# Where the parting copies, transposes and joining copies of gated rows are issued in a decoder layer's SwiGLU

## The chip, the cores and the metric

The kernel runs on one core of a Trainium2 chip. The metric is the device time of one execution in microseconds. The engines are named as the profile names them: PE (TensorE), DVE (VectorE), ACT (ScalarE), POOL (GpSimd) and SP (SyncE, which here only issues DMAs).

## The reference

One decoder layer in fp32 on 256 tokens, with D_MODEL = 2048 and D_FF = 5632:

```python
def swiglu(x, w_gate, w_up, w_down):
    return (jax.nn.silu(x @ w_gate) * (x @ w_up)) @ w_down
...
h = h + 0.5 * swiglu(rmsnorm(h, g_ffn1[l]), w1_gate[l], w1_up[l], w1_down[l])
z = rmsnorm(h, g_mix[l]) @ w_in[l]
y_a = spatial_gating(z[..., :o_q], g_v[l], w_s[l], b_s[l])
y_b = window_attention_sinks(z[..., o_q:o_k], z[..., o_k:o_v], z[..., o_v:], sinks[l])
y = jnp.concatenate([rmsnorm(y_a, g_a_out[l]), rmsnorm(y_b, g_b_out[l])], axis=-1)
h = h + y @ w_out[l]
h = h + cross_attention(rmsnorm(h, g_x[l]), rmsnorm(mem, g_mem[l]), w_xq[l], w_xkv[l], w_xo[l])
h = h + 0.5 * swiglu(rmsnorm(h, g_ffn2[l]), w2_gate[l], w2_up[l], w2_down[l])
return rmsnorm(h, g_final)
```

The change concerns the two SwiGLU blocks, FFN1 and FFN2.

## The kernel before

**Products.** Every fp32 operand x is split into a rounded high part and a low part (`split`, L146 to L148): ACT casts the high part (L147) and DVE subtracts it from x for the low part (L148). A product is then three passes on PE: high by high, low by high, high by low. Tile names say which part is meant: wh and wl are the parts of a weight chunk, th and tl those of sums of weight blocks, afh and afl those of activations.

**Chunks and units.** Weights come in chunks of 1 MB (`load`, L307 ff): one DMA on SP's queue (L318 or L341) fills a raw buffer of which there are three; wh and wl have two buffers each, the sums' tiles one each. A chunk is plain (N), or it is multiplied by one of two Strassen-like schemes (C and S). An S chunk needs sums of its weight blocks: DVE makes them in three steps (L320, L323, L324), and then its halves (T1 with T3, T2 with T4) are split, each with a 1024-wide cast of th on ACT and a 1024-wide subtract of tl on DVE. Its own weights need a 1536-wide cast and subtract, those of N and C chunks 2048-wide ones. Eight chunks make a unit, whose products accumulate in PSUM banks (matmuls at L411). In FFN1 the gate and up products are 11 units c = 0 to 10 (tiles f1g...): unit 0 has plain chunks, units 2 to 9 the kinds "SCSCSCSC". FFN2 (f2g...) has 11 units of C and S chunks. The down products are four units of each FFN (f1d..., f2d...), with the kinds of `KINDS_D`.

**What sets the order.** `push` loads a chunk and calls `turn` with the chunk's matmuls; `turn` emits the matmuls of the chunk before and, at a unit's end, what follows from its result. `turn` also keeps the list `later`: an entry (n, f) has f called n chunks after it was put there, 0 meaning at once in the same turn. So a unit's end is worked off in the first chunks of the next unit, which are called its head here. The order on PE is pinned as it is written. The order on ACT, DVE, POOL and SP is made by a scheduler from the order of the code and its dependencies, so an instruction can be issued earlier or later than it is written.

**From a gate unit to the down products.** At a gate unit's end, DVE and ACT combine its banks (L561 to L572), apply SiLU (L688) and multiply by the up half (L692 or L694). The result is gated rows of two token blocks, 128 tokens each, with tokens on partitions. The down products need them with channels on partitions. `rows_done` (L655 to L685) does this for each unit: per token block a parting copy on ACT (L664, tile f1w or f2w) separates the 16-bit halves of the fp32 numbers, and a transposing DMA on SP's queue (L669, tile f1t or f2t) turns them; then four joining copies on ACT (L677, tile f1a or f2a), one for each of two halves q and two token blocks, put the halves together again. Each q makes one chunk of activations, `acts[2 * c + q]`, which `inner` takes in the down stage (and for the first few already in unit 10): `fill` (L200 ff) adds or subtracts its blocks and splits it into afh and afl. Before the change both parting copies and both transposes are written at a unit's end (`later` 0) and all four joins two chunks later (`later` 2).

**FFN1's beginning.** In units 0 and 1 of FFN1 the normalized input n1 is still being prepared beside the products: activations at L249 and L910, casts and subtracts of n1fh and n1fl.

Of the kernel before, what the change touches and what calls it, by code (L numbers as in the profile page):

```python
# [10 lines left out]
U16 = mybir.dt.uint16  # L11
# [6 lines left out]
TB = 2  # L18
# [15 lines left out]
def layer_kernel(  # L34
# [22 lines left out]
    nc = tc.nc  # L57
# [13 lines left out]
    def nm(s):  # L71
        uid[0] += 1
        return f"{s}_{uid[0]}"

    def m4(s):
        return mid.tile([P, 1024], F32, tag="m4", name=nm(s))

    def s2(s):
        return tmp.tile([P, 512], F32, tag="s2", name=nm(s))
# [39 lines left out]
    h = const.tile([P, TB, D], F32, name="h")  # L119
# [103 lines left out]
    def laid(kind, k, tb):  # L223
        return BASE[kind].index(f"A{tb + 1}{k + 1}")
# [234 lines left out]
    later = []  # L459
# [95 lines left out]
    KINDS_D = "NNSNSNSN" + "NSNSNSN" + "NNSNSNN"  # L555
# [96 lines left out]
    def ffn(s, get, rs, wgu, wd, on_block, first=None, on_token_block=None):  # L652
        acts = [None] * 22
        pairs = [None] * 22

        def rows_done(c, rows_):
            a = m4(s + "a")
            words = a.bitcast(U16).rearrange("p (q i t h) -> p q i t h", q=2, i=4, h=2)
            halves_ = []

            def turned():
                for tb in range(TB):
                    w = s2(s + "w").bitcast(U16)
                    nc.scalar.copy(  # L664
                        w.rearrange("p (h c) -> p h c", h=2),
                        rows_[tb].bitcast(U16).rearrange("p (c h) -> p h c", h=2),
                    )
                    t = s2(s + "t").bitcast(U16)
                    nc.sync.dma_start_transpose(t.rearrange("p (b r) -> p b r", b=8), w)  # L669
                    halves_.append(t.rearrange("p (h b t) -> p b t h", h=2, b=4))  # L670

            def joined():
                for q in range(2):
                    kind = KINDS_D[2 * c + q]
                    for tb in range(TB):
                        i, j = laid(kind, 0, tb), laid(kind, 1, tb)
                        nc.scalar.copy(  # L677
                            words[:, q, i:j + 1:j - i], halves_[tb][:, 2 * q:2 * q + 2]
                        )
                    acts[2 * c + q] = a[:, q * 512:(q + 1) * 512].rearrange(  # L680
                        "p (k t) -> p k t", k=4
                    )

            later.append((0, turned))
            later.append((2, joined))  # L685

        def gated(up, sg, r, tb):
            nc.scalar.activation(  # L688
# [15 lines left out]
        def gu_unit(c):  # L704
            got = {}

            def late(u):
                r = rs()
                c22 = s2(s + "u")
                at = {(0, 0): got["p1"], (1, 1): c22, (0, 1): got["v"], (1, 0): got["z"]}  # L710
                seven_late(u, got, lambda tb, j: at[tb, j])
                gated(at[0, 1], (at[0, 0], at[0, 0]), r, 0)
                gated(c22, (at[1, 0], at[1, 0]), r, 1)
                rows_done(c, (at[0, 0], at[1, 0]))

            kinds = MORE if 2 <= c <= 9 else FEWER
            order = range(8)
            if c == (first is not None):
                order = ORDER[first is None]
            u = Unit(s + "g", "".join(kinds[j] for j in order))  # L720
            for i in range(8):
                push(
                    u, i, wgu[order[i], c], lambda j=order[i]: get(j),
                    lambda i=i: (
                        i == u.kinds.rindex("S") and seven_early(u, got), i == 7 and late(u)
                    ),
                    beside=lambda i: (
                        first[2](8 + i) if first is not None and c == 1
                        else rs() if (c, i) == (0, 5) else inner(i - 5) if c == 10 and i >= 5 else None
                    ),  # L730
                )

        def plain_gu_unit(c):
            pairs_, before, prep, rs0 = first
            u = Unit(s + "g", "N" * 8, alone=(7,))
            u.gate_first = True

            def late():
                r = rs0()
                sg = [s2(s + "sg") for _ in range(TB)]  # L740
                for tb, (g, up) in enumerate((("P2", "Q3"), ("Q4", "R"))):
                    gated(u[up], (u[g], sg[tb]), r, tb)
                rows_done(c, sg)

            pieces = {0: (1, 0, 3, 2), 1: (1, 3, 0, 2)}
            for i in range(8):
                push(
                    u, i, wgu[i, c], lambda i=i: have(pairs_, i), late if i == 7 else None,
                    pieces=pieces.get(i), beside=prep, before=before,
                )  # L750
# [747 lines left out]
```

## Time and profile before

| | us |
|---|---|
| median of three timed runs (2054.82 to 2057.21) | 2055.46 |
| the profiled execution | 2053.67 |
| its span, first to last instruction | 2051.8 |
| granted TensorE clock, as a share of full speed | 0.999 |
| HBM read, MB | 398.52 |
| DVE busy in tl subtracts of FFN1's gate units (L148, 76 of 1219 ns) | 92.5 |
| ACT idle ahead of the joins of FFN1, waiting for f1t (9 times) | 20.1 |
| ACT idle ahead of the joins of FFN2, waiting for f2t (10 times) | 10.2 |

The profile follows one execution. A row of a timeline has the start, the duration, the engine, the line in the code, the operation and its tiles, and in brackets how long the engine had been idle just before and what ended that idle time. Durations of neighbouring instructions on ACT and DVE overlap a little at their ends, so the distance between two starts is somewhat less than a duration. PEld is the loading of weights into TensorE, beside PE's matmuls.

### The profile page before, as it was taken

The page shows a single profiled execution, that of the slowest core. Times are in us where ns is not written, and L with a number is a line of the kernel's source. Part 1 is how long each engine was busy: PE and PEld are TensorE (multiplying, and loading weights), DVE is VectorE, ACT ScalarE, POOL GpSimd, SP SyncE. Part 2 cuts the span into 40 slices and gives each one's busy share as a digit, 9 for nine tenths or more (in the row PEclk, how much of TensorE's full clock was granted, in tenths as well). Part 3 has the DMA queues.
Part 4 walks back from the last instruction along what each step waited for, and adds up shares of the span by engine and source line. Part 5 has one row for each costly group of instructions (what it writes and reads, how often), then busy time and mean ns, then how long its engine had stood idle before and what let it go on. Part 6 is the DMA issues. An engine that isn't in the chain of part 4 may idle for free.

```text
span 2051.8 us, 24290 instructions
## 1 busy us (share of the span) xinstructions
PE 2021.7 (99%) x9235; PEld 1672.0 (81%) x9235; DVE 1859.9 (91%) x1998; ACT 1293.0 (63%) x1432; POOL 34.4 (2%) x57
## 2 busy tenths in 40 slices
PE   9999999999999999999999999999999999999998
PEld 8777777778888888888888888888888888888886
DVE  6999999989998987989888987799999999999988
ACT  7866666666655675655546765676666667675554
POOL 0000000000000010200000000000000000000000
PEclk9999999999999999999999999999999999999999
DMA  8566666566555565544555553556666666656563
GB/s 312 191 202 219 202 209 213 188 216 215 207 202 207 200 240 179 200 176 168 186 187 186 183 176 134 185 179 221 215 210 231 215 215 207 234 200 219 186 220 129
DMA packets 106884, 413.72 MB, mean 202 GB/s; under 512 B 53376, under 2 KB 55440, under 8 KB 59664
## 3 DMA queue, kind: packets, MB, share of 16 engines
q1 hardware_dynamic: 104320, 405.04, 56.7%
q0 software_dynamic: 2016, 6.30, 0.9%
q8 instruction: 72, 1.18, 0.2%
q10 hardware_dynamic: 432, 0.84, 0.1%
q14 instruction: 44, 0.36, 0.0%
HBM read 398.52 MB, written 2.10 MB: 195 GB/s over the span
## 4 chain that ended last, share of the span: by engine, by line
PE 85%; DVE 5%; ACT 5%; DMA 3%; issue 2%; SPq 0%; POOL 0%; POOLq 0%; DVEq 0%; ACTq 0%
PE f2gQ L411 14%; PE f1gQ L411 11%; PE f2dQ L411 6%; PE f1dQ L411 5%; PE f2gP L411 5%; PE f1gP L411 4%; PE xqQ L411 3%; PE f2dP L411 3%; PE f1dP L411 2%; PE woQ L411 2%; PE xoQ L411 2%; PE f2dR L411 2%; ACT f1gwh L147 2%; PE vQ L411 2%; PE mv0Q L411 2%
## 5 line engine op out<-in xcount | busy, mean ns | idle before, releaser
L148 DVE TENSOR_TENSOR f1gwl<-f1gw,f1gwh 128x1536 fp32r<-128x1536 f32 (+2 forms) x94 | 181.8, 1935 | 37.6 <-ACT f1gwh L147 37.0
L148 DVE TENSOR_TENSOR f2gwl<-f2gw,f2gwh 128x1536 fp32r<-128x1536 f32 (+1 forms) x88 | 179.2, 2038 | 8.1 <-ACT f2gwh L147 7.5
L147 ACT CAST f2gwh<-f2gw 128x1536 fp32r<-128x1536 f32 (+1 forms) x88 | 150.6, 1711 | 48.9 <-PE f2gQ L411 32.6
L147 ACT CAST f1gwh<-f1gw 128x1536 fp32r<-128x1536 f32 (+2 forms) x94 | 153.0, 1628 | 40.8 <-PE f1gQ L411 14.7
L147 ACT CAST f1gth<-f1gt 128x1024 fp32r<-128x1024 f32 x76 | 79.7, 1051 | 90.4 <-DVE f1gt L320 59.0
L411 PE MATMUL f2gQ<-f2gwh,n4fh 128*128 128x512 f32 x317 | 123.7, 390 | 0.2 <-DVE f2gv L570 0.2
L411 PE MATMUL f2gQ<-f2gwh,n4fl 128*128 128x512 f32 x317 | 123.4, 389 | 0.0
L147 ACT CAST f2gth<-f2gt 128x1024 fp32r<-128x1024 f32 x82 | 85.2, 1049 | 56.0 <-DVE f2gt L324 30.7
L147 ACT CAST f2dwh<-f2dw 128x2048 fp32r<-128x2048 f32 (+1 forms) x44 | 77.3, 1758 | 58.5 <-PE f2dQ L411 37.3
L411 PE MATMUL f1gQ<-f1gwh,n1fl 128*128 128x512 f32 x286 | 111.4, 390 | 1.6 <-DVE n1fl L148 1.6
L411 PE MATMUL f1gQ<-f1gwh,n1fh 128*128 128x512 f32 x286 | 111.6, 390 | 0.0
L147 ACT CAST f1dwh<-f1dw 128x2048 fp32r<-128x2048 f32 (+1 forms) x44 | 77.2, 1757 | 49.0 <-PE f1dQ L411 31.6
L148 DVE TENSOR_TENSOR f1dwl<-f1dw,f1dwh 128x2048 fp32r<-128x2048 f32 (+1 forms) x44 | 92.0, 2093 | 10.1 <-ACT f1dwh L147 10.0
L148 DVE TENSOR_TENSOR f2dwl<-f2dw,f2dwh 128x2048 fp32r<-128x2048 f32 (+1 forms) x44 | 92.1, 2093 | 10.0 <-ACT f2dwh L147 9.9
L148 DVE TENSOR_TENSOR f2gtl<-f2gt,f2gth 128x1024 fp32r<-128x1024 f32 x82 | 99.8, 1220 | 1.0
L411 PE MATMUL f2gQ<-f2gwl,n4fh 128*128 128x512 f32 x317 | 96.6, 389 | 0.0
L148 DVE TENSOR_TENSOR f1gtl<-f1gt,f1gth 128x1024 fp32r<-128x1024 f32 x76 | 92.5, 1219 | 2.3 <-ACT f1gth L147 1.7
L411 PE MATMUL f1gQ<-f1gwl,n1fh 128*128 128x512 f32 x286 | 86.9, 389 | 0.0
L411 PEld LDWEIGHTS f2gQ<-f2gwh,n4fh 128*128 128x128 f32 x317 | 59.5, 188 | 12.9 <-DVE f2gv L570 0.6
L411 PEld LDWEIGHTS f2gQ<-f2gwh,n4fl 128*128 128x128 f32 x317 | 59.5, 188 | 12.4
L411 PEld LDWEIGHTS f2gQ<-f2gwl,n4fh 128*128 128x128 f32 x317 | 59.4, 188 | 12.3
L411 PE MATMUL f1gQ<-f1gth,n1fh 128*128 128x512 f32 x152 | 60.1, 395 | 8.7 <-ACT f1gth L147 8.7
(823 smaller groups left out, 6067.1 us busy)
## 6 DMA issues: line engine op xcount, KB each, us to landing
f2gw<-in_w_gu SPq DMA_DIRECT2D x88, 1024.0 KB, 4.9
f1gw<-in_w_gu SPq DMA_DIRECT2D x86, 1024.0 KB, 4.9
f1dw<-in_w_down SPq DMA_DIRECT2D x44, 1024.0 KB, 4.8
f2dw<-in_w_down SPq DMA_DIRECT2D x44, 1024.0 KB, 4.8
wow<-in_w_out SPq DMA_DIRECT2D x16, 1024.0 KB, 4.9
xqw<-in_w_xq SPq DMA_DIRECT2D x16, 1024.0 KB, 4.8
xow<-in_w_xo SPq DMA_DIRECT2D x16, 1024.0 KB, 4.8
qw<-in_w_in SPq DMA_DIRECT2D x8, 1024.0 KB, 4.8
```

The source lines that it names most:

```text
L147: nc.scalar.copy(hi, src)
L148: nc.vector.tensor_tensor(lo, src, hi.bitcast(F32), ALU.subtract)
L411: nc.tensor.matmul(self.banks[name], x, y, start=name not in self.begun, stop=self.left[name] == 0)
```

## The change

The code in `rows_done` is divided by token block and by half. The parting copy and the transposing DMA of token block tb are now written 1 + tb chunks after the unit's end, and the two joining copies of half q 4 + q chunks after it. Number and shape of the operations stay as they are.

```diff
-            def turned():
+            def turned(tb):
+                w = s2(s + "w").bitcast(U16)
+                nc.scalar.copy(
+                    w.rearrange("p (h c) -> p h c", h=2),
+                    rows_[tb].bitcast(U16).rearrange("p (c h) -> p h c", h=2),
+                )
+                t = s2(s + "t").bitcast(U16)
+                nc.sync.dma_start_transpose(t.rearrange("p (b r) -> p b r", b=8), w)
+                halves_.append(t.rearrange("p (h b t) -> p b t h", h=2, b=4))
+
+            def joined(q):
+                kind = KINDS_D[2 * c + q]
                 for tb in range(TB):
-                    w = s2(s + "w").bitcast(U16)
-                    nc.scalar.copy(
-                        w.rearrange("p (h c) -> p h c", h=2),
-                        rows_[tb].bitcast(U16).rearrange("p (c h) -> p h c", h=2),
-                    )
-                    t = s2(s + "t").bitcast(U16)
-                    nc.sync.dma_start_transpose(t.rearrange("p (b r) -> p b r", b=8), w)
-                    halves_.append(t.rearrange("p (h b t) -> p b t h", h=2, b=4))
-
-            def joined():
-                for q in range(2):
-                    kind = KINDS_D[2 * c + q]
-                    for tb in range(TB):
-                        i, j = laid(kind, 0, tb), laid(kind, 1, tb)
-                        nc.scalar.copy(
-                            words[:, q, i:j + 1:j - i], halves_[tb][:, 2 * q:2 * q + 2]
-                        )
-                    acts[2 * c + q] = a[:, q * 512:(q + 1) * 512].rearrange(
-                        "p (k t) -> p k t", k=4
-                    )
-
-            later.append((0, turned))
-            later.append((2, joined))
+                    i, j = laid(kind, 0, tb), laid(kind, 1, tb)
+                    nc.scalar.copy(words[:, q, i:j + 1:j - i], halves_[tb][:, 2 * q:2 * q + 2])
+                acts[2 * c + q] = a[:, q * 512:(q + 1) * 512].rearrange("p (k t) -> p k t", k=4)
+
+            for tb in range(TB):
+                later.append((1 + tb, lambda tb=tb: turned(tb)))
+            for q in range(2):
+                later.append((4 + q, lambda q=q: joined(q)))
```

Since the new code is four lines shorter, later lines have numbers lower by four, and the parting copy, the transpose and the join stand at L663, L668 and L675. The order on PE and POOL is the same in both kernels. On the other engines the scheduler's order changes at these places.

On ACT, in the head of FFN1's gate unit 3 (units 2 to 9 read alike), before: the two parting copies of unit 2's rows (f1w), joins (f1a) among the casts of th and wh for unit 3's first chunks (f1gth, f1gwh).

```order
L664 COPY f1w_245_1270<-f1gp1_232_1211 128x1024
L664 COPY f1w_247_1274<-f1gz_234_1213 128x1024
L677 COPY f1a_244_1269<-f1t_246_1272 128x2x256
L147 CAST f1gth_263_1322<-f1gt_262_1316 128x1024
L677 COPY f1a_244_1269<-f1t_248_1276 128x2x256
...
L147 CAST f1gwh_268_1359<-f1gw_267_1358 128x2048
L147 CAST f1gth_265_1326<-f1gt_262_1316 128x1024
L147 CAST f1gwh_271_1386<-f1gw_270_1385 128x1536
```

The two rows left out are the joins of the second half. The same place after:

```order
L663 COPY f1w_255_1304<-f1gp1_232_1211 128x1024
L663 COPY f1w_265_1350<-f1gz_234_1213 128x1024
L675 COPY f1a_244_1269<-f1t_256_1306 128x2x256
L147 CAST f1gth_261_1318<-f1gt_260_1312 128x1024
L147 CAST f1gwh_268_1355<-f1gw_267_1354 128x2048
L675 COPY f1a_244_1269<-f1t_266_1352 128x2x256
L675 COPY f1a_244_1269<-f1t_256_1306 128x2x256
L147 CAST f1gth_263_1322<-f1gt_260_1312 128x1024
L147 CAST f1gwh_271_1382<-f1gw_270_1381 128x1536
L675 COPY f1a_244_1269<-f1t_266_1352 128x2x256
```

The parting copies and the first join keep their places; the 2048-wide cast moves ahead of three joins, and the last join moves behind the 1536-wide cast. In these units the order on SP stays as it was: two transposes, then a weight load.

On SP, in FFN1's gate unit 1, where unit 0's rows are transposed, the two transposes among the weight loads (f1gw) before:

```order
L318 DMA f1gw_589<-in_w_gu 128x2048
L341 DMA f1gw_654<-in_w_gu 128x2048
L669 DMA_TRANSPOSE f1t_529<-f1w_527 128x8x128
L669 DMA_TRANSPOSE f1t_533<-f1w_531 128x8x128
L318 DMA f1gw_722<-in_w_gu 128x2048
L341 DMA f1gw_787<-in_w_gu 128x2048
L318 DMA f1gw_830<-in_w_gu 128x2048
L341 DMA f1gw_872<-in_w_gu 128x2048
```

and after:

```order
L318 DMA f1gw_585<-in_w_gu 128x2048
L341 DMA f1gw_650<-in_w_gu 128x2048
L318 DMA f1gw_718<-in_w_gu 128x2048
L341 DMA f1gw_785<-in_w_gu 128x2048
L668 DMA_TRANSPOSE f1t_583<-f1w_581 128x8x128
L318 DMA f1gw_830<-in_w_gu 128x2048
L668 DMA_TRANSPOSE f1t_648<-f1w_646 128x8x128
L341 DMA f1gw_872<-in_w_gu 128x2048
```

The pair moves two loads back, and a load stands between its two. In this unit the joins and n1's casts and activations on ACT change places too.

On DVE, in the first down unit of FFN2 (the subtracts of dwl, dtl and of the activations' afl), before:

```order
L324 TENSOR_TENSOR f2dt_14717<-f2dt_14717,f2dw_14713 128x512
L148 TENSOR_TENSOR f2dtl_14724<-f2dt_14717,f2dth_14723 128x1024
L148 TENSOR_TENSOR f2afl_14831<-f2a_12612,f2afh_14830 128x512
L148 TENSOR_TENSOR f2afl_14916<-f2a_12612,f2afh_14915 128x512
L148 TENSOR_TENSOR f2dwl_14757<-f2dw_14755,f2dwh_14756 128x2048
L148 TENSOR_TENSOR f2dtl_14728<-f2dt_14717,f2dth_14727 128x1024
```

and after:

```order
L148 TENSOR_TENSOR f2dtl_14724<-f2dt_14717,f2dth_14723 128x1024
L324 TENSOR_TENSOR f2dt_14717<-f2dt_14717,f2dw_14713 128x512
L148 TENSOR_TENSOR f2afl_14831<-f2a_12612,f2afh_14830 128x512
L148 TENSOR_TENSOR f2dwl_14757<-f2dw_14755,f2dwh_14756 128x2048
L148 TENSOR_TENSOR f2dtl_14728<-f2dt_14717,f2dth_14727 128x1024
L148 TENSOR_TENSOR f2afl_14916<-f2a_12612,f2afh_14915 128x512
```

One afl moves from ahead of dwl to behind dtl. At the same place of FFN1 the 2048-wide dwl moves from behind the second dtl to ahead of it. In the gate units of FFN2 the orders stay the same but for the ends of units 0 and 9, where a wh cast on ACT moves ahead of the last join.

## The prediction

> **What bounds the kernel now.** First the profile's page: its span
>
> ```profile
> span 2051.8 us, 24290 instructions
> ```
>
> and the engines' busy times.
>
> ```profile
> PE 2021.7 (99%) x9235; PEld 1672.0 (81%) x9235; DVE 1859.9 (91%) x1998; ACT 1293.0 (63%) x1432; POOL 34.4 (2%) x57
> ```
>
> PE (TensorE) is busy for all but some 30 us, so an edit that leaves PE's own work alone can only win back waits. What PE waits for is in the waits view (total us, times, longest):
>
> ```profile
> PE f1gQ L411 <- ACT f1gth L147: 8.7, 8, 2.4
> PE f1gQ L411 <- DVE f1gtl L148: 6.9, 8, 0.9
> ```
>
> 8.7 + 6.9 = 15.6 us lie in the gate units of FFN1, eight times each: once per unit from unit 2 to unit 9. The table of windows shows one such unit of FFN1, from a row of its sums to the same row a unit later, and beside it one of FFN2 (columns: us; busy PE, PEld, DVE, ACT, POOL with counts; clock; DMA share; GB/s).
>
> ```profile
> 199.70:242.80 43.10, 41.38 (x180) 33.63 (x180) 40.05 (x38) 27.08 (x26) 0.00 (x0) 1.00 0.63 207
> 1609.30:1650.30 41.00, 41.00 (x182) 33.74 (x181) 40.19 (x38) 27.46 (x26) 0.00 (x0) 1.00 0.62 218
> ```
>
> The same work takes 43.10 and 41.00: FFN1 loses 2.10 per unit, and DVE (40.05) would allow most of that back. Where the loss arises is in the head of a unit, read from the timelines of one (unit 3): start, duration, and in brackets what the engine waited for. SP's transposes, then ACT:
>
> ```profile
> 147.19 2.60 SPq L669 DMA_TRANSPOSE f1t<-f1w  x2
> ```
>
> ```profile
> 150.42 0.68 ACT L677 COPY f1a<-f1t 128x512 uint16<-128x512 uint16 x1 [2.31 <-DMA f1t<-f1w]
> 151.01 1.04 ACT L147 CAST f1gth<-f1gt 128x1024 fp32r<-128x1024 f32 x1
> 151.96 1.83 ACT L677 COPY f1a<-f1t 128x512 uint16<-128x512 uint16 x3
> 153.70 1.91 ACT L147 CAST f1gwh<-f1gw 128x2048 fp32r<-128x2048 f32 x1
> 155.51 1.04 ACT L147 CAST f1gth<-f1gt 128x1024 fp32r<-128x1024 f32 x1
> ```
>
> DVE, then PE:
>
> ```profile
> 153.23 0.68 DVE L324 TENSOR_TENSOR f1gt<-f1gt,f1gw 128x512 f32<-128x512 f32 x1
> 155.64 2.29 DVE L148 TENSOR_TENSOR f1gwl<-f1gw,f1gwh 128x2048 fp32r<-128x2048 f32 x1 [1.72 <-ACT f1gwh L147]
> 157.85 1.22 DVE L148 TENSOR_TENSOR f1gtl<-f1gt,f1gth 128x1024 fp32r<-128x1024 f32 x1
> ```
>
> ```profile
> 155.32 0.39 PE L411 MATMUL f1gQ<-f1gth,n1fl 128*128 128x512 f32 x1
> 156.59 0.50 PE L411 MATMUL f1gQ<-f1gth,n1fh 128*128 128x512 f32 x1 [0.89 <-ACT f1gth L147]
> 156.93 0.39 PE L411 MATMUL f1gQ<-f1gth,n1fl 128*128 128x512 f32 x1
> ...
> 157.63 0.63 PE L411 MATMUL f1gQ<-f1gtl,n1fh 128*128 128x512 f32 x2
> 159.12 0.74 PE L411 MATMUL f1gQ<-f1gtl,n1fh 128*128 128x512 f32 x2 [0.86 <-DVE f1gtl L148]
> 159.69 0.40 PE L411 MATMUL f1gP<-f1gwh,n1fh 128*128 128x512 f32 x1
> ```
>
> Read it as one chain. ACT's first joining copy waits 2.31 us for the transposing DMA; behind it stand the first th cast, three more joins (1.74 from start to next start) and a 2048-wide gwh cast, and only then the second th cast, at 155.51. PE wanted that at 155.55 (155.32 plus the spacing of matmuls, 157.63 − 156.93 = 0.70 over three, some 0.23) and starts at 156.59: 1.04 late, plus 0.11 of refilling, since the next start is 0.34 later instead of 0.23. The same gwh holds up gwl on DVE by 1.72, gwl stands ahead of the second tl, and so PE waits again: 159.12 instead of 157.63 + 2 × 0.23 = 158.09, 1.03 late, plus 0.12. Together 2.30 per head, which is the 2.1 of the windows within reading.
>
> **The change: heads of units 3 to 9.** The copies and transposes keep their places on ACT and SP here, although the code issues them one and two chunks past the end; what moves is the joins. gwh now stands directly behind the first th cast, one join less is ahead of the second th, and the last join lies behind the next gwh. Step by step, with the durations above: join at 150.42 as before (same DMA), th at 151.01, gwh at 151.96 and, 1.81 later, at 153.77 two joins of 0.58 each (1.74 / 3), then the second th at 154.93, 0.58 earlier than 155.51. It can be used at 156.01 (156.59 − 0.58): PE is 0.46 late plus 0.11, 0.57 instead of 1.15. On DVE gwl starts when L324 is through, 153.23 + 0.68 = 153.91, since gwh ends at 153.87; the second tl follows 2.21 later (157.85 − 155.64), from 156.12 to 157.34. PE reaches it at 156.01 + 0.34 + 3 × 0.23 + 2 × 0.23 = 157.50: the second wait is gone by a slack of 0.16. The saving is 0.58 + 1.15 = 1.73 per head; seven heads make 12.1.
>
> This needs gwh to be free to start at 151.96, 1.74 before it did. Its buffer comes free with the last product that reads it. A later cast of ACT in the same unit shows when that is:
>
> ```profile
> 163.57 1.91 ACT L147 CAST f1gwh<-f1gw 128x2048 fp32r<-128x2048 f32 x1 [0.54 <-PE f1gQ L411]
> ```
>
> It is released by PE after the hi products of the chunk that begins at 159.69 (16 × 0.23 = 3.6 on from there is 163.3) and not at that chunk's end, two us later. By the same rule the buffer in the head comes free at about 151. The remainder of a unit hangs on PE and only shifts. The last join, now later, is read by nobody before the down stage; it costs nothing.
>
> **Unit 1 and the head of unit 2.** Here copies and transposes do move: each transpose now stands alone on SP, behind a weight load each, and joins lie where n1f's casts were. Unit 1's wait on DVE and PE:
>
> ```profile
> 66.40 0.68 DVE L148 TENSOR_TENSOR n1fl<-n1f,n1fh 128x512 fp32r<-128x512 f32 x1
> 67.14 0.50 PE L411 MATMUL f1gQ<-f1gwh,n1fl 128*128 128x512 f32 x1 [1.58 <-DVE n1fl L148]
> ```
>
> Unit 2's head, SP with the last load and the pair of transposes, then PE:
>
> ```profile
> 94.63 0.33 SPq L341 DMA_DIRECT2D f1gw<-in_w_gu  x1
> 102.51 2.61 SPq L669 DMA_TRANSPOSE f1t<-f1w  x2
> ```
>
> ```profile
> 113.42 0.50 PE L411 MATMUL f1gQ<-f1gth,n1fh 128*128 128x512 f32 x1 [2.40 <-ACT f1gth L147]
> ```
>
> The joins of unit 0 that stood ahead of the gwh on which n1fl hangs go behind it; at most one is directly ahead of it (0.58), so n1fl gains up to half a us. Against this, three joins now stand ahead of a later gwh in the same unit (1.74), where DVE may be late by about 1. Unit 2's head gains the 1.73 if its transposes land as they did. I take +1.0 for the two (ends −1.5 and +2.3). How long a transpose takes to land is in the rows of its tile: for unit 2's pair,
>
> ```profile
> DMA to landing us min/median/max: 4.3/4.5/4.7
> ```
>
> for units 3 to 9,
>
> ```profile
> DMA to landing us min/median/max: 3.0/3.2/3.2
> ```
>
> and for units 1 to 9 of FFN2, where one of a pair can stand behind a weight load:
>
> ```profile
> DMA to landing us min/median/max: 3.0/3.2/6.9
> ```
>
> [...] In unit 1 the change puts each transpose behind a load; at 6.9 both would still land before their joins, which the code puts two and more chunks (43.1 / 8 = 5.4 us each) later.
>
> **The first down unit.** The fill of the activations is now spread, so one afl subtract less stands ahead of dwl and tl in FFN2; in FFN1 dwl passes ahead of the second tl.
>
> ```profile
> 1845.44 1.29 DVE L148 TENSOR_TENSOR f2afl<-f2a,f2afh 128x512 fp32r<-128x512 f32 x2
> 1850.12 0.73 PE L411 MATMUL f2dQ<-f2dtl,f2afh 128*128 128x512 f32 x2 [0.90 <-DVE f2dtl L148]
> ```
>
> ```profile
> 518.88 1.22 DVE L148 TENSOR_TENSOR f1dtl<-f1dt,f1dth 128x1024 fp32r<-128x1024 f32 x1
> 521.13 1.07 PE L411 MATMUL f1dQ<-f1dtl,f1afh 128*128 128x512 f32 x4
> ```
>
> The first product of FFN1 that waits for a dwl:
>
> ```profile
> 522.96 0.50 PE L411 MATMUL f1dP<-f1dwl,f1afh 128*128 128x512 f32 x1 [0.31 <-DVE f1dwl L148]
> ```
>
> FFN2: two afl take 1.29 together, so dwl and tl come some 0.6 earlier against a wait of 0.90: 0.6 won (0.3 to 1.0). FFN1: the 0.31 goes, but the second tl, if dwl takes its place at 518.88, ends at 518.88 + 2.2 + 1.22 = 522.3 (2.2 for a 2048-wide subtract, 157.85 − 155.64) and PE needs it at 521.13 + 2 × 0.23 = 521.6; it may also be just in time if the order above it shortens. I take 0 (−0.8 to +0.4). FFN2's gate units keep their order but for one join behind a gwh at the ends of two, where PE does not wait: nothing.
>
> **Sum.** 12.1 + 1.0 + 0.6 + 0 = 13.7. The profiled execution took 2053.67, which is its span of 2051.8 and 1.9 around it, and comes to 2040.0; the median of the three timed runs is 2055.46, 1.8 above, and comes to 2041.8.
>
> **The rivals.** A, the whole loss goes: FFN1's heads run as FFN2's. For it: the two windows hold equal work. Then 8 × 2.10 = 16.8, and up to 1.6 of n1fl's wait and 0.6 in FFN2's down unit: 19.0, 2036.5. Against: the step sum still leaves the second th 0.46 late. Chance 0.10.
>
> B, gwh cannot start at 151.96, because its buffer comes free only with the end of PE's chunk, about 152.6 to 153. Then the second th comes at 155.57 or later instead of 155.51; only the second wait goes, since gwl still starts one us earlier: about 0.7 to 1.1 per head, 6 to 9 in all, 2047. Against: the row at 163.57. Chance 0.09.
>
> C, it does nothing that shows: parting copies and transposes stay where they were in eight heads, the first join goes on waiting 2.31, and DVE, 40.05 of 43.10 busy, hands back later in the unit what it won in the head (its slack at 43.10 − 1.73 = 41.37 is 1.3). Then 2055.5. Against: FFN2 runs at 41.00 with 40.19 on DVE. Chance 0.06.
>
> D, slower: the transposes land later. The first join stands ahead of both th casts, so each us of landing is a us of PE per head. With the 1.73 won, this decides from 3.2 + 1.73 = 4.9 us after issue. At the 6.9 of FFN2 it is 3.7 more, 2.0 net per head over seven or eight heads, 14 to 16 in all: about 2070. For it: 4.7 at 102.51. Against, in units 3 to 9 the last load ahead of the pair has landed before it is issued at 147.19:
>
> ```profile
> 139.52 0.34 SPq L341 DMA_DIRECT2D f1gw<-in_w_gu  x1
> f1gw<-in_w_gu SPq DMA_DIRECT2D x86, 1024.0 KB, 4.9
> ```
>
> 139.52 + 4.9 = 144.4, and nothing brings that load later relative to the unit's end. Chance 0.05.
>
> **How the numbers follow.** The forecast has 0.70. Its own ends: 13.7 − 2.5 − 0.3 − 0.8 = 10.1 and 13.7 + 1.3 + 0.4 + 0.4 = 15.8, so 2039.7 to 2045.4. Leaving out C and D (0.11) and part of B's upper end, the range is 2036 to 2049. About 0.2%, 4.1 us, is what a measurement of this kernel can tell from no change. Faster by more than that: the forecast, A, B and a little of C, 0.88; within it, the rest of C and the poorest B, 0.07; slower, D, 0.05.
>
> **What would show it.** Right: PE's waits for f1gth fall to some 0.3 each (8.7 to about 3), those for f1gtl vanish, gwl's 1.72 idle on DVE vanishes, and a unit of FFN1 takes 41.4; f2dtl's 0.90 falls to 0.3. A new wait for f1dtl may appear. Wrong: a gwh cast in the head released by PE later than 151.96 of this frame (B), joins that wait over 2.31 (D), or new waits of PE for gwl, tl or t behind the head (C).

## The result and the profile after

The changed kernel takes 2042.03 us, the median of four runs (2039.93 to 2042.97), against 2055.74 before (2054.82 to 2057.21). The ratio is 0.9931 with an interval of 0.9914 to 0.9948. A second set of runs gave 2041.35 and 0.9933 (0.9919 to 0.9948). In the profiled executions it is 2041.79 against 2053.67.

The page of the changed kernel: its span

```profile
span 2040.0 us, 24281 instructions
```

and the waits of PE (total us, times, longest):

```profile
PE f1gQ L411 <- ACT f1gth L147: 4.4, 8, 2.1
PE f1gQ L411 <- ACT n1r L249: 2.2, 1, 2.2
PE xoQ L411 <- ACT n4r L249: 1.2, 1, 1.2
PE f1gQ L411 <- DVE n1fl L148: 1.2, 1, 1.2
```

The eight waits for f1gtl (6.9 us) are gone, those for f1gth have halved, and there is a new wait of 2.2 us for n1r. Unit 3's head shows the first two; this is the place that the prediction worked through. SP, ACT, DVE and PE in the changed kernel:

```profile
149.24 2.61 SPq L668 DMA_TRANSPOSE f1t<-f1w  x2
```

```profile
152.46 0.68 ACT L675 COPY f1a<-f1t 128x512 uint16<-128x512 uint16 x1 [2.29 <-DMA f1t<-f1w]
153.04 1.05 ACT L147 CAST f1gth<-f1gt 128x1024 fp32r<-128x1024 f32 x1
154.00 1.91 ACT L147 CAST f1gwh<-f1gw 128x2048 fp32r<-128x2048 f32 x1
155.81 1.26 ACT L675 COPY f1a<-f1t 128x512 uint16<-128x512 uint16 x2
156.97 1.05 ACT L147 CAST f1gth<-f1gt 128x1024 fp32r<-128x1024 f32 x1
```

```profile
155.26 0.68 DVE L324 TENSOR_TENSOR f1gt<-f1gt,f1gw 128x512 f32<-128x512 f32 x1
155.94 2.29 DVE L148 TENSOR_TENSOR f1gwl<-f1gw,f1gwh 128x2048 fp32r<-128x2048 f32 x1
158.14 1.22 DVE L148 TENSOR_TENSOR f1gtl<-f1gt,f1gth 128x1024 fp32r<-128x1024 f32 x1
```

```profile
157.37 0.39 PE L411 MATMUL f1gQ<-f1gth,n1fl 128*128 128x512 f32 x1
158.07 0.50 PE L411 MATMUL f1gQ<-f1gth,n1fh 128*128 128x512 f32 x1 [0.32 <-ACT f1gth L147]
...
159.11 1.09 PE L411 MATMUL f1gQ<-f1gtl,n1fh 128*128 128x512 f32 x4
160.03 0.40 PE L411 MATMUL f1gP<-f1gwh,n1fh 128*128 128x512 f32 x1
```

The first join still waits 2.29 us for its DMA. gwh starts right behind the first th, with no release to wait for; gwl follows L324 with no gap; PE is 158.07 − 157.37 − 0.23 = 0.47 late for the second th and runs its four tl products in one go. A unit, from one row of the table of windows:

```profile
181.99:223.45 41.46, 41.11 (x181) 33.67 (x181) 40.20 (x38) 27.15 (x25) 0.00 (x0) 1.00 0.64 216
```

41.46 instead of 43.10. Since PE's order is the same in both kernels (9235 products each), product n of the one can be set against product n of the other, and the difference of their starts says where time was won or lost. In us against the kernel before:

| stretch | changed | predicted |
|---|---|---|
| unit 1 of FFN1 | +3.67 | with the next, −1.0 |
| unit 2 | −1.51 | |
| unit 3 | −1.69 | −1.73 |
| units 4 to 9 | −10.25 | −10.4 |
| first down unit of FFN1 | −0.71 | 0 |
| gate units of FFN2 | −0.13 | 0 |
| first down unit of FFN2 | −0.99 | −0.6 |
| whole span | −11.8 | −13.7 |

What went wrong in unit 1 is in these rows of the changed kernel: SP's load and the first transpose behind it, and how long that took to land;

```profile
60.70 0.33 SPq L341 DMA_DIRECT2D f1gw<-in_w_gu  x1
61.24 1.36 SPq L668 DMA_TRANSPOSE f1t<-f1w  x1
```

```profile
DMA to landing us min/median/max: 6.1/6.1/6.1
```

ACT's second parting copy, and the n1r activation behind it, for which PE waits:

```profile
67.36 1.05 ACT L663 COPY f1w<-f1sg 128x1024 uint16<-128x1024 uint16 x1 [1.90 <-DMA f1t<-f1w]
68.31 0.40 ACT L147 CAST n1fh<-n1f 128x256 fp32r<-128x256 f32 x1
68.62 1.47 ACT L147 CAST f1gwh<-f1gw 128x1536 fp32r<-128x1536 f32 x1
69.99 0.83 ACT L249 ACTIVATE n1r<-n,sm 128x256 f32<-128x256 f32 x2
```

```profile
70.87 0.50 PE L411 MATMUL f1gQ<-f1gth,n1fh 128*128 128x512 f32 x1 [2.17 <-ACT n1r L249]
```

and two windows of 3.41 us, the one with that wait and the one behind it (the first number after the length is PE's busy time, the one after all busy times the granted clock):

```profile
68.59:72.00 3.41, 1.24 (x6) 0.95 (x6) 2.31 (x3) 3.41 (x6) 0.00 (x0) 1.00 0.92 288
72.00:75.41 3.41, 3.41 (x10) 2.63 (x9) 3.38 (x8) 3.41 (x8) 0.00 (x0) 0.50 0.67 235
```

61.24 + 6.1 = 67.34: the second parting copy writes the scratch buffer that the first transpose is still reading, and starts when that has landed. It holds up ACT by 1.90, and n1r with it; PE waits 2.17 (2.3 with refilling) and then runs at half clock for 3.41 us, which costs another 1.6. With 0.4 won at n1fl (66.61 now for 67.14 before, of which 0.1 was won ahead of unit 1) these make 3.5 of unit 1's 3.67.

### The profile page after: what moved, and what is told of

Read it like the earlier page. It is cut to its first block, busy times and chain, and to the rows that moved or that the text cites. A ratio compares the mean times of both kernels' runs of the same rounds, so it can differ in the third digit from the quotient of the medians.

```text
span 2040.0 us, 24281 instructions
## 1 busy us (share of the span) xinstructions
PE 2020.9 (99%) x9235; PEld 1673.9 (82%) x9235; DVE 1861.1 (91%) x1998; ACT 1293.9 (63%) x1432; POOL 34.4 (2%) x57
## 4 chain that ended last, share of the span: by engine, by line
PE 94%; ACT 3%; DVE 2%; issue 1%; DMA 0%; POOL 0%; POOLq 0%; DVEq 0%; ACTq 0%
PE f2gQ L411 15%; PE f1gQ L411 14%; PE f2dQ L411 6%; PE f1dQ L411 6%; PE f2gP L411 6%; PE f1gP L411 5%; PE xqQ L411 3%; PE f2dP L411 3%; PE f1dP L411 3%; PE woQ L411 2%; PE xoQ L411 2%; PE f2dR L411 2%; PE f1dR L411 2%; PE vQ L411 2%; PE mv0Q L411 2%; PE mv1Q L411 2%
## 5 line engine op out<-in xcount | busy, mean ns | idle before, releaser
L411 PE MATMUL f2gP<-f2gwh,n4fh 128*128 128x512 f32 x176 | 68.7, 390 | 0.0
```

The lines of the kernel that those rows point to most:

```text
L411: nc.tensor.matmul(self.banks[name], x, y, start=name not in self.begun, stop=self.left[name] == 0)
```

## The experiments

**Only the joins.** The transposes as before, the joins as in the change. (In all diffs minus is the changed kernel.)

```diff
-                later.append((1 + tb, lambda tb=tb: turned(tb)))
+                later.append((0, lambda tb=tb: turned(tb)))
```

> Parting copies and transposes as before, both blocks at the unit's end; only the joins are moved, to four and five chunks. Theory: the joins' places on ACT make the whole gain of the heads, and the issue of the transposes makes the loss in unit 1. Then FFN1's units 3 to 9 take 41.45 us as in the changed kernel, PE's wait for n1r (2.2) and the half clock behind it are gone, and the time is 2042.0 less 3.9 = about 2038. Rival 1: part of the heads' gain comes from transposes that are spread out; then the units take between 41.5 and 43.2, and the time lies between 2042 and 2054. Rival 2: unit 1 loses by the later joins among n1's casts, not by the transposes; then the wait for n1r stays, and the time is 2042.

2039.83, ratio 0.9923 (0.9907 to 0.994). Units 3 to 9 take what they take in the changed kernel; one is, by two entries of the chain a unit apart,

```profile
179.60 4.08 PE f1gQ L411 x18
221.03 4.08 PE f1gQ L411 x18
```

41.43, so the gain of the heads needs nothing of what was done to the transposes. The wait for n1r and the half clock in unit 1 are gone: unit 1 stands at −0.26 against before, 3.9 better than in the changed kernel. Both rivals fall. The time is 2 above the expected 2038. In the profiled execution most of that is half clock at another place: around and behind unit 2's wait of 1.9 for f1gth the windows show

```profile
110.58:114.00 3.42, 1.50 (x7) 1.11 (x7) 3.37 (x3) 3.42 (x5) 0.00 (x0) 1.00 0.73 235
114.00:117.41 3.41, 3.41 (x10) 2.73 (x9) 3.38 (x3) 0.95 (x2) 0.00 (x0) 0.50 0.90 380
```

and unit 2 gains nothing (−0.02). The rest is in the two first down units, which gain 0.82 here and 1.70 in the changed kernel.

**Only the transposes.**

```diff
-                later.append((4 + q, lambda q=q: joined(q)))
+                later.append((2, lambda q=q: joined(q)))
```

> Only the parting copies and transposes are moved, one and two chunks past the end; all four joins stand two chunks past it, as before. Theory: the heads gain nothing (43.16 us a unit, waits for f1gth and f1gtl as before), unit 1 loses the 3.4 us that it lost in the changed kernel, so about 2055.7 + 3.4 = 2059, slower than before. Rival 1 (spreading the transposes helps the heads): units below 43, time under 2055. Rival 2 (unit 1's loss comes from the joins): 2055.7.

2057.73, ratio 1.0016 (1.0006 to 1.0025): slower than before by 3.4 (2054.34 in the same set), as expected. The waits of PE:

```profile
PE f1gQ L411 <- ACT f1gth L147: 9.1, 8, 2.8
PE f1gQ L411 <- DVE f1gtl L148: 6.9, 8, 0.9
PE f1gQ L411 <- DVE n1fl L148: 1.9, 1, 1.9
PE f1gQ L411 <- ACT n1r L249: 1.8, 1, 1.8
```

The heads are as before (units 4 to 9 differ by +0.06 in all), and unit 1 loses 3.94 with the joins where they were. The profiled execution is one of the slowest of the ten (2059.20) and loses 3.05 in unit 2 as well: its wait for f1gth is 2.8 there, behind it 12 products of the chain take 4.15 us where 12 take 2.72 elsewhere, and the granted clock of this execution is 0.996. So the parts separate: joins give, transposes take. FFN1's first down unit, however, gains 0.81 here and 0.21 with the joins alone.

**A tile of its own for unit 0's parting copies.**

```diff
+            ws = m4(s + "ws") if c == 0 and s == "f1" else None
...
-                w = s2(s + "w").bitcast(U16)
+                w = (ws[:, tb * 512:(tb + 1) * 512] if c == 0 and s == "f1" else s2(s + "w")).bitcast(U16)
```

> The changed kernel, but in unit 0 of FFN1 the two parting copies write halves of a tile of their own, so that the second does not wait for the first transpose to have read its scratch buffer. The transposes stay one and two chunks past the end, each near a weight load on SP's queue. Theory: it is the second copy's wait on ACT that delays n1r; then PE's wait for n1r and the half clock go, 2042.0 less 3 to 4 = 2038 to 2039. Rival: the transposes' place on SP behind loads is enough, or the later joins are; then a wait of about 2 us stays in unit 1 and the time is 2042.

2035.99, ratio 0.9906 (0.9891 to 0.9921): 6 below the changed kernel's time, 5 by the ratios, and 2 to 3 better than expected. The wait for n1r is down to 0.2, though the transposes are still spread between loads (at 56.2 and 61.9) and f1t takes up to 7.8 to land in this run. What is left:

```profile
PE f1gQ L411 <- DVE f1gtl L148: 2.9, 7, 1.8
PE xoQ L411 <- ACT n4r L249: 1.2, 1, 1.2
```

A caution belongs to it: with one scratch tile fewer the scheduler ordered the heads differently too. ACT now has a parting copy, th, the other parting copy, gwh, join, th; there is no wait for f1gth at all, one of about 0.2 for f1gtl in its place, and units take 41.3. That, and unit 2 (−3.89), make it better than the removed wait alone: of the 6.0 between the profiled executions, units 3 to 9 have 1.6, unit 2 has 2.4 and unit 1 has 1.4. Unit 1 still loses 2.28, since a wait of 1.8 for f1gtl near its end is followed by half clock as well (products 0.43 us apart instead of 0.23).

**Joins on POOL.** Unit 0's copies and transposes at its end, the joins on another engine.

```diff
-                later.append((1 + tb, lambda tb=tb: turned(tb)))
+                later.append((1 + tb if c else 0, lambda tb=tb: turned(tb)))
...
-                    nc.scalar.copy(words[:, q, i:j + 1:j - i], halves_[tb][:, 2 * q:2 * q + 2])
+                    nc.gpsimd.tensor_copy(words[:, q, i:j + 1:j - i], halves_[tb][:, 2 * q:2 * q + 2])
```

> Unit 0's copies and transposes at its end as before, all else as in the changed kernel, and the joins are done by POOL instead of ACT. Theory: what is left of the heads' waits (0.3 each, 2.1 in unit 2) is the first join's wait for the transposing DMA in ACT's queue; without it the heads wait for nothing and FFN1's units take 41.0 as FFN2's do: 2038 less 7 x 0.45 less 2.1 = about 2033. Rival: POOL's copies slow DVE or ACT beside them, so the 1024-wide tl subtract takes longer than 1.22 us and the units take 41.5 or more: 2038 or slower.

2054.65, ratio 0.9996 (0.9987 to 1.0005): the rival. No wait for f1gth is left, but others have come:

```profile
PE f2gQ L411 <- DVE f2gv L570: 4.9, 7, 0.9
PE f1gQ L411 <- DVE f1gtl L148: 4.0, 9, 0.5
```

The four joins of unit 3 on POOL (count; shortest, median and longest in ns; first and last start), and what DVE does near their end:

```profile
L675 POOL COPY f1a<-f1t x4: 1127/1408/10164, 149.5 to 161.7; 128x512 uint16<-128x512 uint16 x4
```

```profile
159.16 1.04 DVE L323 TENSOR_TENSOR f1gt<-f1gt,f1gw 128x512 f32<-128x512 f32 x1
160.23 1.04 DVE L324 TENSOR_TENSOR f1gt<-f1gt,f1gw 128x512 f32<-128x512 f32 x1
161.19 1.69 DVE L148 TENSOR_TENSOR f1gtl<-f1gt,f1gth 128x1024 fp32r<-128x1024 f32 x1
```

The first join lasts 10.2 us, until 159.65. DVE runs without a gap and at its usual durations until 159.13, so the join ends 0.5 behind DVE's first idle moment. The other three take 1.1 to 1.7 us where ACT needs 0.68, and DVE's steps beside them take longer: 1.04 for 0.68 and 1.69 for 1.22. A gate unit's DVE work grows from 40.20 to 41.51 us, which is nearly all of the unit, as a window over one shows:

```profile
196.13:237.88 41.75, 41.28 (x181) 33.64 (x180) 41.51 (x38) 25.22 (x22) 13.93 (x5) 1.00 0.63 215
```

In the head itself, PE waits 0.47 for the second tl with no join on ACT: behind the DMA wait, DVE's own order (gwl ahead of the second tl) is next. Set against the kernel before, FFN1's units 2 to 9 still gain 12.2; unit 1 loses 1.8, FFN2's gate units lose 6.7 and the two first down units 2.5, so that nothing is left.

**Two joins at two, two at four.** As the joins alone, but

```diff
-                later.append((4 + q, lambda q=q: joined(q)))
+                later.append((2 + 2 * q, lambda q=q: joined(q)))
```

> As the run with only the joins moved, but the first half's two joins stand two chunks past the unit's end and the second half's four. In the heads of FFN1's units 3 to 9 ACT then has join, th, join, gwh, join, th: as many joins ahead of the second th as in the changed kernel, but gwh one join (0.58 us) later. Theory (gwh's place sets the second wait, the number of joins the first): the wait for f1gth stays at 0.3, gwl starts some 0.5 later and the wait for f1gtl comes back with about 0.4 plus 0.1 per head, units of 41.9 to 42.0: 2039.8 plus 4 = about 2044. Rival (only the joins ahead of the second th count): units of 41.45, 2039.8.

2045.69, ratio 0.9953 (0.9938 to 0.9968). DVE and PE in unit 3's head:

```profile
156.99 2.29 DVE L148 TENSOR_TENSOR f1gwl<-f1gw,f1gwh 128x2048 fp32r<-128x2048 f32 x1 [0.57 <-ACT f1gwh L147]
159.19 1.22 DVE L148 TENSOR_TENSOR f1gtl<-f1gt,f1gth 128x1024 fp32r<-128x1024 f32 x1
```

```profile
158.53 0.50 PE L411 MATMUL f1gQ<-f1gth,n1fh 128*128 128x512 f32 x1 [0.35 <-ACT f1gth L147]
160.47 0.74 PE L411 MATMUL f1gQ<-f1gtl,n1fh 128*128 128x512 f32 x2 [0.27 <-DVE f1gtl L148]
```

The first wait is as in the changed kernel (0.35), the second is back (0.27 idle), and units 4 to 9 gain 7.33 instead of 10.49, 0.53 less each. gwh's place on ACT sets the second wait, the joins ahead of the second th the first, as the prediction's sum had it. The rest of the difference to the joins alone is in unit 1, where PE waits 2.1 for n1fl and nine products of the chain take 3.33 us, 0.37 each instead of 0.23 (+4.28).

**The last two gate units' joins as before.** As the joins alone, but

```diff
-                later.append((4 + q, lambda q=q: joined(q)))
+                later.append((4 + q if c < 9 else 2, lambda q=q: joined(q)))
```

> As the run with only the joins moved, but the joins of the last two gate units (9 and 10) stand two chunks past the end as before. Theory: the gains of the first down units (0.7 in FFN1, 1.0 in FFN2) come from these joins alone, since with them the order on DVE there is the old one: the waits for f1dwl (0.3) and f2dtl (0.9) come back, the heads stay as they were, 2039.8 plus 1.7 = 2041.5. Rival: the down units gain from what lies ahead of them (buffers that come free earlier); then 2039.8.

2040.66, ratio 0.9929 (0.9914 to 0.9944). FFN2's first down unit loses its gain (+0.03 against before, where the joins alone have −0.61), and the wait for f2dtl is back at 0.9; a new wait at this unit's start costs it another 0.46, which is not in the +0.03. In FFN1 nothing changes (−0.17 against −0.21): the theory holds for FFN2 and fails for FFN1, whose gain in the changed kernel (−0.71) comes with the transposes, as the run with only those (−0.81) says too; by which step was not tried. Half clock is missing in unit 2 here although PE's wait there is 1.8, close to the 1.9 with the joins alone, and unit 2 gains 1.84 (the last section sets the two waits side by side).

**The own tile, and unit 0 as before.**

```diff
+            ws = m4(s + "ws") if c == 0 and s == "f1" else None
...
-                w = s2(s + "w").bitcast(U16)
+                w = (ws[:, tb * 512:(tb + 1) * 512] if c == 0 and s == "f1" else s2(s + "w")).bitcast(U16)
...
-                later.append((1 + tb, lambda tb=tb: turned(tb)))
+                later.append((1 + tb if c else 0, lambda tb=tb: turned(tb)))
```

> The own tile for unit 0's parting copies, with unit 0's copies and transposes at its end as before; the others as in the changed kernel. Theory: neither the wait for n1r nor unit 2's long wait for f1gth is there, and no half clock follows: about 2035. Rival: unit 1 waits elsewhere (as the 1.8 for f1gtl in the run with the own tile) and the time is 2036 to 2038.

2036.28, ratio 0.9908 (0.9892 to 0.9925), no different from the own tile alone; unit 1 loses the same 2.28, by the same wait of 1.8 for f1gtl. The rival holds. It is 5 better than the changed kernel of the same set, the next run: its slowest execution took 2037.56, the fastest of the changed kernel 2040.84.

**The changed kernel again.**

> The changed kernel again, beside the others on one chip: 2042, with the wait of about 2 us for n1r in unit 1. If the half clock behind that wait depends on when the wait falls and not on its length, it may be missing here, which gives about 1.6 us less.

2041.35. The wait for n1r is 1.8, and unit 1 stands at +3.26. That is 0.41 below the +3.67 of the first profile, and the shorter wait (1.8 for 2.17) makes 0.37 of it, so by this estimate the 1.6 of the half clock has not gone.

## Why the prediction was right, and where it was wrong

**The heads of units 3 to 9** held step for step: 1.73 forecast, 1.69 in unit 3 and 10.25 / 6 = 1.71 in the others, 11.9 for seven against 12.1. PE was to be 0.46 late for the second th and is 0.47 late; the second wait was to go by a slack of 0.16, and the run with joins at two and four, which puts gwh one join later, brings it back. The release of gwh's buffer, on which rival B rested, came early enough: gwh starts right behind th.

**Unit 1 and the head of unit 2** is the term that failed: +1.0 was taken, −2.2 came (3.67 lost, 1.51 won), beyond even its lower end of −1.5. n1fl's gain came as forecast (0.4), and the loss of about 1 to three joins ahead of a later gwh did not: behind the half clock unit 1 moves by 0.1 only. The step that failed is the sentence that both transposes, at 6.9, would still land before their joins. They do, but the joins are not the only ones that wait for a transpose: the second parting copy writes the buffer that the first transpose reads, and stands on ACT ahead of n1r. The landing time itself was foreseen (6.9 was taken, 6.1 came). Who waits for it is what the prediction had wrong. That the buffer is the cause rests on the row at 67.36, on the run with only the transposes, where the same copy waits 1.91 for the same DMA and PE 1.8 for n1r, and on the own tile, which takes the wait away but reorders the heads too. What the wait cost beyond itself, 1.6 of half clock, was nowhere in the sum.

**Unit 2's pair of transposes** landed at 4.5 to 5.0, slow as before, and the head won 1.51 instead of 1.73. Why they are slow, the prediction left open. The traces show one packet on the queue of instructions beside the pair (DMA queues of the kernel before, 102.0 to 105.7):

```profile
q1 hardware_dynamic: 1511, 0.38, 69.7%
q8 instruction: 1, 0.02, 2.1%
```

2.1% of 16 engines for 3.7 us are 1.2 us of one engine, about what the pair is late. The packet lies in that window in all eight profiles whose pair takes 4.3 or more, and in neither of the two with the own tile, whose pair lands as those of units 3 to 9 did before:

```profile
DMA to landing us min/median/max: 3.1/3.2/3.2
```

That is ten of ten, but no run moved the packet alone, so the cause is not shown. It also answers rival D in small: in the changed kernel unit 2's first join waits 1.8 longer for its DMA than unit 3's (4.07 against 2.29), and PE's wait there is 2.07 against 0.32, 1.75 more. There the later landing cost PE one for one (1.75 for 1.78); it only happens once.

**The down units.** In FFN2 0.99 against 0.6: the wait of 0.90 goes altogether, with its refilling, because DVE comes to the afl earlier as well. In FFN1 0.71 against 0: the 0.31 for dwl goes as forecast, and the second tl, now behind dwl, is just in time (DVE, then PE),

```profile
508.29 2.29 DVE L148 TENSOR_TENSOR f1dwl<-f1dw,f1dwh 128x2048 fp32r<-128x2048 f32 x1
510.49 1.22 DVE L148 TENSOR_TENSOR f1dtl<-f1dt,f1dth 128x1024 fp32r<-128x1024 f32 x1
```

```profile
511.37 1.12 PE L411 MATMUL f1dQ<-f1dtl,f1afh 128*128 128x512 f32 x4
```

ending at 511.71 where PE needs it at 511.37 + 2 × 0.23 = 511.8, so it costs nothing; the price of 0.7 that the simple bound gave does not arise.

**The sum.** 13.7 was forecast and the profiled executions differ by 11.9: the term of unit 1 and unit 2 came out 3.2 worse than taken, the first down units 1.1 better, and the heads of units 3 to 9 0.2 worse. That the median lands on the forecast (2042.03 against 2041.8) owes something to chance: the profiled execution of before lay 2.1 below its median of 2055.74, that of the changed kernel only 0.2 below its own, so the medians differ by 13.7. The profiled execution of before has no half clock, that of the changed kernel has 3.41 us of it.

**Rival A** (all of the heads' loss goes) fell for the reason found on POOL: without the DMA wait DVE is next, by 0.2 to 0.5. **B** and **C** fell with the rows of unit 3.

## What to carry to other kernels

When a step is moved, list everything that waits for its DMAs, not only the step that uses the result: a buffer in a rotating pool is waited for by whoever writes it next (here a parting copy, for 1.90 us), and that instruction may stand in front of unrelated work (here n1r, for which PE then waited 2.17). Where the head of a queue waits for a DMA, look also at what stands behind it: moving one 1.8 us cast ahead of copies that nobody needs yet gave 1.7 us per unit with the DMA wait untouched. And test the halves of such a change apart, since here one half gave some 14 us and the other took 3.

## What the runs showed of the hardware

The length of a wait alone did not decide whether half clock followed it. In the changed kernel the clock is half from 72.00 to 75.41, behind the wait of 2.17 for n1r, and it is full behind unit 2's wait of 2.07 for f1gth. With the joins alone it is half from 114.00 to 117.41, behind unit 2's wait of 1.9 (shown above); with the old joins at the end it is full from 108 to 120, around a wait of 1.8. The wait of 2.40 in unit 2 of the kernel before is the longest of the five, and up to PE's last product that trace has no half clock at all.

In the changed kernel's trace the half clock lasts 3.41 us, and its beginning and end lie 19 and 20 times that length behind the first record of the clock, 7.15 us into the span. If the time is divided in such steps, PE is busy for 1.24 us in the step with the wait of 2.17, and for 1.61 in the one that has most of the wait of 2.07. With the joins alone, 1.50 is around the wait of 1.9 (shown above), and with the old joins at the end 1.67 around the wait of 1.8:

```profile
110.56:113.98 3.42, 1.67 (x8) 1.35 (x8) 3.37 (x3) 3.42 (x5) 0.00 (x0) 1.00 0.80 266
```

In the kernel before, where the first record of the clock lies at 6.90, the wait of 2.40 is divided between two steps:

```profile
109.30:112.71 3.41, 1.72 (x8) 1.10 (x6) 1.69 (x3) 3.41 (x5) 0.00 (x0) 1.00 0.54 187
112.71:116.13 3.42, 1.87 (x7) 1.25 (x8) 3.42 (x3) 2.03 (x2) 0.00 (x0) 1.00 0.62 254
```

So half clock followed the two steps with 1.24 and 1.50 and none of the four with 1.61, 1.67, 1.72 and 1.87. That it hangs on PE's busy time in a step is the author's reading of these five waits and was not shown: no run moved a wait against the steps on purpose, and the busy time of PE is rough, since its ends are modelled. The 3.41 us of half clock in the changed kernel cost PE 1.6: its products start 1.90 later than in the kernel before ahead of them, and 3.51 later behind them.

Of the 19 executions of the kernel before that were timed beside the joins alone, the seven with a granted clock of 0.997 took 2055.57 to 2058.55, and the twelve with 0.998 or 0.999 took 2053.30 to 2054.64; where half clock fell in them no trace was kept to show.

In unit 3 with the joins on POOL, the first copy of 16-bit halves stood for 10.2 us while DVE ran without a gap at its usual durations, and ended 0.5 us behind DVE's first idle moment. The copies after it took 1.1 to 1.7 us each, and DVE's subtracts and adds were 39 to 53% longer beside them. The profile's spans on POOL are rough.
